# The last product of each layer in quarters (token half by column half), with gates and late attention blocks moved into existing memory

## The chip, the cores and the metric

One core of a Trainium2 chip runs the whole program. The metric is the time of one execution on the device in microseconds; lower is better. TensorE appears as PE (its weight loads as PEld), VectorE as DVE, ScalarE as ACT, GpSimd as POOL, and SyncE, which issues every DMA here, as SP.

## The reference

Two layers, each with a 1024 x 1024 residual stream (1024 tokens, width 1024), and a final RMSNorm. Cut to what matters:

```python
def hybrid_layer(x, c_act, norm_g, w_ada, b_ada, w_in, w_out, pos):
    shift, scale, gate = jnp.split(c_act @ w_ada + b_ada, 3, axis=-1)
    h = rms_norm(x, norm_g) * (1.0 + scale[:, None, :]) + shift[:, None, :]
    rq, rk, rv, rg, sq, sk, sv, sg = jnp.split(h @ w_in, split_at, axis=-1)   # 8 x 512 columns
    y_ret = retention(rotary(rq), rotary(rk), rv)           # 4 heads x 128
    y_ret = merge_heads(y_ret) * jax.nn.silu(rg)
    y_sb = stick_breaking(sq, sk, sv)                       # 8 heads x 64, strictly causal
    y_sb = merge_heads(y_sb) * jax.nn.silu(sg)
    y = jnp.concatenate([y_ret, y_sb], axis=-1) @ w_out
    return x + gate[:, None, :] * y
```

The stick-breaking attention multiplies, for a query t and a key s, sigmoid(q.k) by the product of (1 - sigmoid(q.k)) over the keys between s and t: a running product over keys, from the query backwards.

## The kernel before

**Arithmetic.** Every large product is done in three float16 passes, high x high, high x low and low x high (`three`, L605), each 128 x 128 by 512 columns. A tile of output takes 8 pieces of depth (k) times three passes, 24 matmuls. Activations live as `hh` and `hl` (high and low), weights as tiles `w` of 8 per group.

**Layer.** `layers` (L1124) goes through four head pairs: `stick_project` gives queries, keys, values and gates of two stick-breaking heads, `retention_project` one retention head in 8 token blocks with its chunk recurrences. Then `out_project` (L1002) multiplies the concatenated `y` with W_out: first the left 512 columns (hf = 0) for the token tiles t = 0 to 7, then the right 512 (hf = 1) for t = 0 to 7. `residual` (L1037) scales by the gate row, adds to the residual x on DVE and stores to DRAM; `finish` (L1108) normalises a complete row, and `h_chunk` turns four token tiles into `hh` and `hl` of the next layer. The matmuls of tile t need `("yr", l, k, t)` for k below 4, and for k from 4 on `("ys", l, k - 4, t // 4)`: the attention output of head pair k - 4 for that half of the tokens. `ys` of the second half exists only when query blocks 4 to 7 of that pair are through.

**Attention.** `attend` (L732) takes the eight blocks b of 128 queries of one head pair. For a block, PE forms the scores `z`, ACT the two sigmoids `beta` and `keep`, DVE runs for either head j a scan over the keys (`keep`), a product (`beta`) and, after ACT has copied the high part, a subtraction for the low part (`head_block`, L779); SP then issues transposing DMAs of `keep` into `ta`. `weigh` (L822) multiplies `ta` with the values into `av`, two blocks at a time (0 and 1, 2 and 3, 4 and 5, 6 and 7), and the half's result times its gate `sg` becomes `y`. A block with b of 4 or more needs four of the six `f4` buffers (`room4`), so blocks 4 to 7 follow each other closely in the same buffers.

**Order.** There is no fixed schedule: the generators above run in a planner (`Flow`) which keeps a priced clock per engine and always advances the stream of the lowest rank (DRAIN first, MAIN last) that can go on. What it emits is the static order of each engine's instructions; on the chip an engine takes them in that order and waits on semaphores. `Room` objects count buffers: `roomw` weight tiles (13), `roomst` staging tiles of loaded weights (3), `roomfl` value buffers (2), `rooms` the gates `sgs` (2). A weight tile is loaded into staging, split into high and low by ACT and DVE, and given back when the group's last tile has read it. A line L83 in the profile is the recorder through which all instructions pass, so tiles and shapes tell them apart.

## Time and profile before

| | |
|---|---|
| median of 3 runs | 1134.33 us (1131.88 to 1135.35) |
| the profiled execution's own time | 1132.87 us |
| its span, first to last instruction | 1131.0 us |
| PE busy | 1040.9 us, 92% of the span |
| DVE busy | 891.7 us, 79% |
| ACT busy | 553.1 us, 49% |
| POOL busy | 261.8 us, 23% |
| mean granted clock of TensorE | 0.983 of full |

The profiled execution lies 1.46 us below the median, and 1.87 us of it lie outside the span. Full granted clock is 2.4 GHz, 0.50 is 1.2 GHz. Layer 0's last product begins at 483.9 us of the span, layer 1's at 1011.1; the latter ends the program.

### The profile page before, as it was taken

What the parts mean: (1) busy time and instruction counts of PE and PEld (TensorE: products, weight loads), DVE (VectorE), ACT (ScalarE), POOL (GpSimd) and SP (SyncE); (2) the same over time, 40 slices, a digit from 0 to 9 for tenths busy, and PEclk for the clock granted to TensorE, in tenths of its full rate; (3) what the DMA queues carried; (4) which work ended last, traced back from release to release, by engine and by line L of the source; (5) the groups of instructions that cost most, each with busy time, mean ns of one, the idle gap of its engine ahead of it and who ended that gap; (6) DMA issues with size and microseconds to landing.
All of it is one profiled execution on the core that took longest, in us unless ns stands there. A gap on an engine that the chain in (4) does not pass through costs nothing. (4 is left out here: it accounts for less than half of the span.)

```text
span 1131.0 us, 18382 instructions
## 1 busy us (share of the span) xinstructions
PE 1040.9 (92%) x6321; PEld 506.3 (45%) x6321; DVE 891.7 (79%) x1689; ACT 553.1 (49%) x1271; POOL 261.8 (23%) x567
## 2 busy tenths in 40 slices
PE   1799989999999999996999999999999999999597
PEld 0444444454444444543455444444444544444343
DVE  6888888899898878975457689988978987887344
ACT  5755554545454646451254555555545464454012
POOL 5731430142014301420010034014302420230002
PEclk9899999999999999998999999999999999999799
DMA  9727675776774756374651566674556365467354
GB/s 279 234 65 154 140 152 132 183 143 157 162 171 89 145 90 140 61 185 114 207 153 57 128 146 137 149 150 82 134 107 124 72 143 109 97 143 168 81 186 162
DMA packets 339164, 156.44 MB, mean 138 GB/s; under 512 B 227904, under 2 KB 315008, under 8 KB 339072
## 3 DMA queue, kind: packets, MB, share of 16 engines
q1 hardware_dynamic: 339072, 155.29, 58.4%
q8 instruction: 49, 0.80, 0.3%
q14 instruction: 43, 0.35, 0.1%
HBM read 90.22 MB, written 10.49 MB: 89 GB/s over the span
## 5 line engine op out<-in xcount | busy, mean ns | idle before, releaser
L83 PE MATMUL acc<-hh,w 128*128 128x512 f16 x1024 | 324.2, 382 | 4.4 <-DVE w L83 3.2
L83 PE MATMUL acc<-w,hh 128*128 128x512 f16 x1024 | 305.0, 379 | 0.0
L83 PEld LDWEIGHTS <-w 128*128 128x128 f16 x1536 | 145.9, 99 | 183.8 <-issue 19.6
L83 POOL TENSOR_TENSOR t<-t,t 128x128 f32<-128x128 f32 (+1 forms) x192 | 137.3, 729 | 264.2 <-DVE t L83 205.3
L83 PE MATMUL acc<-hl,w 128*128 128x512 f16 x512 | 195.8, 382 | 0.9 <-POOL hl L83 0.9
L83 PE MATMUL acc<-w,hl 128*128 128x512 f16 x512 | 194.0, 379 | 0.0
L83 PE MATMUL acc<-w,y 128*128 128x512 f16 (+1 forms) x792 | 170.2, 373 | 3.3 <-ACT y L83 2.9
L83 PEld LDWEIGHTS <-hh 128*128 128x128 f16 x1024 | 92.6, 98 | 99.4 <-issue 11.4
L83 DVE SCALAR_TENSOR_TENSOR w<-wst,w 128x512 f16<-128x512 f32 x160 | 113.0, 722 | 28.2 <-ACT w L83 27.8
L83 DVE TENSOR_TENSOR_SCAN keep<-keep,own 128x640 f32<-128x640 f32 (+3 forms) x64 | 122.8, 1923 | 11.1 <-ACT keep L83 11.0
L83 ACT ACTIVATE w<-wst 128x512 f16<-128x512 f32 x160 | 97.7, 627 | 65.5 <-DMA wst<-in_w_in_dram 32.6
L83 PEld LDWEIGHTS <-y 128*128 128x128 f16 x792 | 76.2, 98 | 90.3 <-ACT y L83 3.4
L83 ACT CAST t<-t 128x128 f16<-128x128 f32 (+1 forms) x128 | 43.9, 352 | 108.3 <-POOL t L83 60.3
L83 ACT CAST keep<-beta 128x640 f16<-128x640 f32 (+3 forms) x64 | 56.3, 883 | 65.3 <-DVE beta L83 64.9
L83 PE MATMUL av<-ta,vt 128*64 128x256 f16 (+1 forms) x960 | 61.5, 280 | 26.8 <-DMA ta<-keep 26.7
L83 ACT ACTIVATE keep<-z 128x512 f32<-128x512 f32 (+3 forms) x128 | 67.8, 529 | 24.1 <-PE z L83 20.5
L83 PEld LDWEIGHTS <-hl 128*128 128x128 f16 x512 | 50.1, 98 | 60.4
L83 DVE TENSOR_TENSOR keep<-beta,keep 128x640 f16<-128x640 f32 (+3 forms) x64 | 67.0, 1051 | 4.5 <-ACT keep L83 4.0
L83 PEld LDWEIGHTS <-vt 128*64 128x64 f16 x960 | 50.6, 117 | 41.6 <-issue 21.9
L83 ACT ACTIVATE beta<-z 128x512 f32<-128x512 f32 (+4 forms) x128 | 68.5, 535 | 0.0
L83 DVE SCALAR_TENSOR_TENSOR beta<-beta,keep 128x639 f32<-128x639 f32 (+3 forms) x64 | 67.2, 1056 | 0.2
L83 POOL MEMSET both<- 128x1 f32 x64 | 5.3, 97 | 253.9 <-DMA ta<-keep 93.0
(104 smaller groups left out, 1308.7 us busy)
## 6 DMA issues: line engine op xcount, KB each, us to landing
wst<-in_w_in_dram SPq DMA_DIRECT2D x128, 256.0 KB, 3.3
wst<-in_w_ada_dram SPq DMA_DIRECT2D x64, 256.0 KB, 3.1
wst<-in_w_out_dram SPq DMA_DIRECT2D x32, 256.0 KB, 3.4
xt<-x SPq DMA_DIRECT2D x24, 256.0 KB, 4.0
xt<-in_x_dram SPq DMA_DIRECT2D x8, 512.0 KB, 5.8
ada<-in_w_ada_dram SPq DMA_DIRECT2D x8, 512.0 KB, 7.2
ada<-in_w_ada_dram SPq DMA_DIRECT2D x4, 1024.0 KB, 9.2
turn<-in_rot_dram SPq DMA_DIRECT2D x64, 64.0 KB, 2.4
```

The source lines that it names most:

```text
L83: real(*args, **kw)
```

## The change

The last product goes in quarters: tiles 0 to 3 left columns, 0 to 3 right, 4 to 7 left, 4 to 7 right. Both column halves of W_out are resident for it: 16 weight tiles in place of 13, and 4 staging tiles in place of 3. The memory comes from three places. The gates `sg` lie in the part of `y` that their own head pair writes later, so the two `sgs` buffers and their `rooms` count are gone. The value buffer `fl` is single. And query blocks 5 and 6 of the last head pair (p = 3) keep their `beta` and `keep` in a tile `home` that takes the memory of `hh` (block 5) or `hl` (block 6), from the moment that all projections of the layer have been issued (`("through", l)`); the next layer's `h_chunk` waits for their transposes. A complete row of tiles 0 to 3 is no longer in SBUF when its second column half is done: `residual` stores both halves, and `again_whole` loads the row again and finishes it, once the last attention block has taken its buffers (`("taken", l, 3)`). The modulation of the layer (`adapt`: gate row, and in layer 0 the next layer's shift and scale) starts at a new rank SPARE, between ATTEND and MAIN, and is lifted to ADAPT after the second head pair's `stick_project`. The number and shapes of matmuls do not change; the planner's order does, over most of the program.

```diff
     def part(self, a):
         name = a.tensor.name
-        return (name, a.offset) if name in self.big else name
+        return (name, a.offset // self.grain.get(name, 1)) if name in self.big else name
...
+    def lift(self, gen, rank):
+
+        for s in self.streams:
+            if s[2] is gen:
+                s[0] = rank
...
-DRAIN, NORM, FEED, ADAPT, ATTEND, MAIN = range(6)
+DRAIN, NORM, FEED, ADAPT, ATTEND, SPARE, MAIN = range(7)
...
-    N4, NW, NA = 6, 13, 2
-    room4, roomq, roomv, rooms = Room(N4), Room(2), Room(2), Room(2)
+    N4, NW, NA = 6, 16, 2
+    room4, roomq, roomv = Room(N4), Room(2), Room(2)
     roomr, roomw, rooma = Room(3), Room(NW), Room(1)
-    roomfl, roomg, roomy = Room(2), Room(5), Room(2)
-    roomat, roomst, roomt, roomrot = Room(NA), Room(3), Room(4), Room(2)
+    roomfl, roomg, roomy = Room(1), Room(5), Room(2)
+    roomat, roomst, roomt, roomrot = Room(NA), Room(4), Room(4), Room(2)
...
-                st = f2("wst", "wst", 3)
+                st = f2("wst", "wst", 4)
...
-            fl = wk.tile([P, 2, CH], F16, tag="fl", bufs=2, name="fl")
+            fl = wk.tile([P, 2, CH], F16, tag="fl", bufs=1, name="fl")
...
-            sg = wk.tile([P, CH], F32, tag="sgs", bufs=2, name="sg")
+
+            sg = y_of(l)[:, 4 + p, 4 * ch:4 * ch + 4].rearrange("p t a q -> p (t a q)").bitcast(F32)
...
                 acc = yield from project(3, ch, ch == 1)
-                yield (), rooms.has()
-                rooms.n -= 1
                 drain(3, ch, acc)
...
-            yield need, room4.has(2 if b < 4 else 4)
-            room4.n -= 2 if b < 4 else 4
-            flow.spawn(ATTEND, head_pair(l, p, b, at))
+            home = None
+            if p == 3 and b in (5, 6):
+
+                yield [*need, ("through", l)]
+                home = apart(big.tile([P, 4, 1024], F32, tag=("hh", "hl")[b - 5], name="home"))
+                flow.grain[home.tensor.name] = 1024
+            else:
+                yield need, room4.has(2 if b < 4 else 4)
+                room4.n -= 2 if b < 4 else 4
+            flow.spawn(ATTEND, head_pair(l, p, b, at, home))
             if b == 0:
                 flow.spawn(ATTEND, weigh(l, p, at))
+        flow.mark(("taken", l, p))
...
+        elif home is not None:
+            betas, keeps = [home[:, j] for j in range(2)], [home[:, 2 + j] for j in range(2)]
...
-    def out_project(l, hf, xres, xnew, fg):
+    def out_project(l, xres, xnew):
...
+        if last:
+            flow.spawn(NORM, final_row(), [("taken", l, 3)], room4.has())
+        for t0, hf in ((0, 0), (0, 1), (4, 0), (4, 1)):
+            g = ("O", l, hf)
+            fs = slice(hf * 512, (hf + 1) * 512)
+            yield [("w", g, 0)]
+            w = W[g]
+            for t in range(t0, t0 + 4):
+                whole = hf and t0
+                if whole:
+                    xt = yield from whole_tile(l, t)
+                    sp.dma_start(out=xt[:, 0:512], in_=xnew[t][:, 0:512])
+                    sp.dma_start(out=xt[:, 512:], in_=xres[t][:, fs])
+                    xs = xt[:, 512:]
                 else:
...
+                    xs = f2("xh")
+                    sp.dma_start(out=xs, in_=xres[t][:, fs])
...
+                flow.spawn(DRAIN, residual(l, hf, t, acc, xs, xt if whole else None, xnew), [acc, xs])
...
+    def whole_tile(l, t):
+        last = l == DEPTH - 1
+        if t < 6 or last:
+            yield [("taken", l, 3), *(["final"] if last else [])], room4.has()
+            room4.n -= 1
+            return f4("xt")
...
-        yield [xs], None, None, LOADED if hf == 0 else 0
-        if hf == 0 or l + 1 < DEPTH:
+        yield [xs], None, None, LATER if xt is None else 0
+        if xt is None or l + 1 < DEPTH:
             sp.dma_start(out=xnew[t][:, fs], in_=xs)
...
+        elif hf:
+            flow.spawn(NORM, again_whole(l, t, xnew), [("x", l, t, i) for i in range(2)])
+
+    def again_whole(l, t, xnew):
+        xt = yield from whole_tile(l, t)
+        sp.dma_start(out=xt, in_=xnew[t])
+        yield [xt]
+        yield from finish(l, t, xt)
...
-                    flow.spawn(NORM, h_chunk(l + 1, t // 4, [xns[t - 3 + j] for j in range(4)], i, n))
+                    flow.spawn(NORM, h_chunk(l + 1, t // 4, [xns[t - 3 + j] for j in range(4)], i, n),
+                               [("at", l, 3, b, j) for b in (5, 6) for j in range(2)])
...
                 if i == 0:
-                    flow.spawn(ADAPT, adapt(l))
+                    rest = adapt(l)
+                    flow.spawn(SPARE, rest)
+                if i == 1:
+                    flow.lift(rest, ADAPT)
                 yield from retention_project(l, i)
...
+            flow.mark(("through", l))
             xnew = (x1, x2)[l]
-            for hf in range(2):
-                yield from out_project(l, hf, xres, xnew, fg)
+            yield from out_project(l, xres, xnew)
```

**PE, last product of layer 1, at the end of token tile 3.** `acc` is a tile's accumulator, `w_11261` and `w_11916` are the first and the last left-column weight tile before, `w_11255` the last left-column tile and `w_11866` the first right-column tile in the changed kernel. Before:

```order
L83 MATMUL acc_12257<-w_11916,y_7315 128x512
L83 LDWEIGHTS y_7315
L83 MATMUL acc_12290<-w_11261,y_7315 128x512
L83 LDWEIGHTS y_7315
L83 MATMUL acc_12290<-w_11261,y_7315 128x512
```

Changed:

```order
L83 MATMUL acc_12231<-w_11255,y_7018 128x512
L83 LDWEIGHTS y_7018
L83 MATMUL acc_12267<-w_11866,y_7018 128x512
L83 LDWEIGHTS y_7018
L83 MATMUL acc_12267<-w_11866,y_7018 128x512
```

The accumulator that follows tile 3 is tile 4, left, before, and tile 0, right, in the changed kernel. The 21 matmuls of tile 4, left, that need no second-half attention still stand directly ahead of the last weighted sum (`av` from blocks 6 and 7) in both kernels; in the changed one four right-column tiles (96 matmuls) stand ahead of them.

**DVE, layer 0, the end of the attention of the last head pair.** `keep_6071`/`keep_6072` before and `keep_6038`/`keep_6039` in the changed kernel belong to query block 7, heads 0 and 1; `home_5834` is block 6; the `up` and `xh` pair is the residual of the `acc` that it names. Before:

```order
L83 SCALAR_TENSOR_TENSOR up_6141<-acc_6047,gate_948 128x512
L83 TENSOR_TENSOR xh_6045<-xh_6045,up_6141 128x512
L83 SCALAR_TENSOR_TENSOR keep_6071<-keep_6071,own_76 128x1024
L83 SCALAR_TENSOR_TENSOR beta_6069<-beta_6069,keep_6071 128x1023
L83 SCALAR_TENSOR_TENSOR up_6178<-acc_6137,gate_948 128x512
L83 TENSOR_TENSOR xh_6135<-xh_6135,up_6178 128x512
L83 TENSOR_TENSOR keep_6071<-beta_6069,keep_6071 128x8x128
L83 SCALAR_TENSOR_TENSOR keep_6072<-keep_6072,own_76 128x1024
L83 SCALAR_TENSOR_TENSOR beta_6070<-beta_6070,keep_6072 128x1023
L83 TENSOR_TENSOR keep_6072<-beta_6070,keep_6072 128x8x128
```

Changed:

```order
L83 SCALAR_TENSOR_TENSOR keep_6038<-keep_6038,own_76 128x1024
L83 SCALAR_TENSOR_TENSOR up_6240<-acc_6159,gate_961 128x512
L83 TENSOR_TENSOR xh_6157<-xh_6157,up_6240 128x512
L83 SCALAR_TENSOR_TENSOR beta_6036<-beta_6036,keep_6038 128x1023
L83 SCALAR_TENSOR_TENSOR keep_6039<-keep_6039,own_76 128x1024
L83 SCALAR_TENSOR_TENSOR up_6278<-acc_6236,gate_961 128x512
L83 TENSOR_TENSOR xh_6234<-xh_6234,up_6278 128x512
L83 SCALAR_TENSOR_TENSOR beta_6037<-beta_6037,keep_6039 128x1023
L83 TENSOR_TENSOR keep_6038<-beta_6036,keep_6038 128x8x128
L83 TENSOR_TENSOR keep_6039<-beta_6037,keep_6039 128x8x128
L83 SCALAR_TENSOR_TENSOR up_6323<-acc_6274,gate_961 128x512
L83 TENSOR_TENSOR xh_6272<-xh_6272,up_6323 128x512
```

Block 7's passes are in both; in the changed kernel the residuals between them are those of right-column tiles (`acc_6159`, `acc_6236` and `acc_6274` are tiles 1, 2 and 3), and block 6's last pass stands directly ahead. Counting back to the last retention block's first pass, the changed kernel has all passes of blocks 4, 5, 6 and 7 in this stretch, before only part of 6 and all of 7; the other passes of 4 to 6 stood earlier.

**SP, layer 0, the last transposes.** `ta` is filled from `keep` for the last weighted sum; `x1` is the DRAM copy of the residual. Before:

```order
L83 DMA x1_83<-xh_6135 128x512
L83 DMA_TRANSPOSE ta_5996<-keep_6071 128x8x128 x2
L83 DMA_TRANSPOSE ta_6144<-keep_6072 128x8x128 x2
L83 DMA xh_6265<-in_x_dram 128x512
L83 DMA x1_83<-xh_6172 128x512
```

Changed:

```order
L83 DMA x1_83<-xh_6157 128x512
L83 DMA xh_6272<-in_x_dram 128x512
L83 DMA xt_6291<-x1_83 128x1024
L83 DMA x1_83<-xh_6234 128x512
L83 DMA_TRANSPOSE ta_6214<-keep_6038 128x8x128 x2
L83 DMA xh_6317<-in_x_dram 128x512
L83 DMA xt_6338<-x1_83 128x1024
L83 DMA x1_83<-xh_6272 128x512
L83 DMA_TRANSPOSE ta_6249<-keep_6039 128x8x128 x2
```

Before, the four transposes of block 7 stand together. In the changed kernel head 1's two stand behind a store of `xh_6272` (tile 3, right) and behind two reloads of whole rows of `x1` (`xt_6291`, `xt_6338`).

## Rows read from the trace of the kernel before

**Rows 1.** Busy time by engine in two stretches (granted clock, DMA share, GB/s last)

```profile
75.00:500.00 425.00, 408.99 (x2582) 196.06 (x2581) 370.08 (x724) 222.86 (x539) 101.84 (x224) 1.00 0.63 137
575.00:1030.00 455.00, 448.67 (x2808) 217.16 (x2807) 379.47 (x737) 242.36 (x572) 101.24 (x231) 1.00 0.56 122
```

**Rows 2.** Timeline of PE in layer 0's last product: start, length, matmuls [idle before]

```profile
483.77 0.33 PE L83 MATMUL psc<-vd,t 128*128 128x128 f16 x3
...
520.14 0.42 PE L83 MATMUL av<-ta,vt 128*64 128x256 f16 x1 [2.63 <-DMA ta<-keep]
525.98 0.37 PE L83 MATMUL av<-ta,vt 128*64 128x256 f16 x2 [5.42 <-DMA ta<-keep]
527.20 3.92 PE L83 MATMUL av<-ta,vt 128*64 128x128 f16 x45 [0.85 <-DMA ta<-keep]
532.56 27.66 PE L83 MATMUL acc<-w,y 128*128 128x512 f16 x126 [1.44 <-ACT y L83]
```

**Rows 3.** Timeline of PE in layer 1's last product, same columns

```profile
1011.09 0.81 PE L83 MATMUL acc<-w,y 128*128 128x512 f16 x3
...
1022.40 2.35 PE L83 MATMUL av<-ta,vt 128*64 128x256 f16 x36
...
1025.67 13.76 PE L83 MATMUL acc<-w,y 128*128 128x512 f16 x63
1039.36 0.82 PE L83 MATMUL z<-k,q 64*128 64x512 f16 x6
...
1054.28 0.37 PE L83 MATMUL av<-ta,vt 128*64 128x256 f16 x1 [10.54 <-DMA ta<-keep]
1057.10 0.42 PE L83 MATMUL av<-ta,vt 128*64 128x256 f16 x2 [2.44 <-DMA ta<-keep]
1058.30 4.59 PE L83 MATMUL av<-ta,vt 128*64 128x128 f16 x45 [0.79 <-DMA ta<-keep]
1064.33 16.01 PE L83 MATMUL acc<-w,y 128*128 128x512 f16 x72 [1.43 <-ACT y L83]
```

**Rows 4.** Busy time by engine in two stretches of 12.5 us, columns as Rows 1

```profile
520.00:532.50 12.50, 4.71 (x48) 3.90 (x48) 2.23 (x3) 1.66 (x2) 0.00 (x0) 0.60 0.36 76
1050.00:1062.50 12.50, 4.99 (x46) 4.38 (x47) 2.14 (x2) 0.86 (x1) 0.00 (x0) 0.50 0.50 105
```

**Rows 5.** Timeline of DVE, layer 0: last retention block's first pass, last attention pass

```profile
489.03 0.75 DVE L83 TENSOR_TENSOR t<-acc,turn 128x256 f32<-128x256 f32 x2
...
521.48 1.23 DVE L83 TENSOR_TENSOR keep<-beta,keep 128x1024 f16<-128x1024 f32 x1 [1.17 <-ACT keep L83]
```

**Rows 6.** Timeline of DVE, layer 1: the same two places

```profile
1012.10 0.76 DVE L83 TENSOR_TENSOR t<-acc,turn 128x256 f32<-128x256 f32 x2 [0.20 <-DVE yt L83]
...
1049.78 2.36 DVE L83 TENSOR_TENSOR keep<-beta,keep 128x1024 f16<-128x1024 f32 x2
```

**Rows 7.** DVE instructions by shape: total busy, mean ns | idle before

```profile
L83 DVE SCALAR_TENSOR_TENSOR w<-wst,w 128x512 f16<-128x512 f32 x160 | 113.0, 722 | 28.2 <-ACT w L83 27.8
...
L83 DVE TENSOR_TENSOR_SCAN keep<-keep,own 128x1024 f32<-128x1024 f32 x16 | 36.4, 2283 | 9.3 <-ACT keep L83 9.3
...
L83 DVE TENSOR_TENSOR_SCAN keep<-keep,own 128x640 f32<-128x640 f32 x16 | 25.2, 1572 | 1.0 <-ACT keep L83 1.0
...
L83 DVE SCALAR_TENSOR_TENSOR up<-acc,gate 128x512 f32<-128x512 f32 x31 | 21.3, 688 | 37.4 <-PE acc L83 37.3
...
L83 DVE SCALAR_TENSOR_TENSOR beta<-beta,keep 128x1023 f32<-128x1023 f32 x16 | 19.3, 1216 | 0.1
L83 DVE TENSOR_TENSOR keep<-beta,keep 128x1024 f16<-128x1024 f32 x16 | 19.3, 1215 | 1.5 <-ACT keep L83 1.3
...
L83 DVE SCALAR_TENSOR_TENSOR beta<-beta,keep 128x639 f32<-128x639 f32 x16 | 13.6, 854 | 0.0
```

**Rows 8.** DMA issues: count, KB each, median us from issue to landing

```profile
x<-xh SPq DMA_DIRECT2D x16, 256.0 KB, 2.2
...
vt<-fl SPq DMA_TRANSPOSE x16, 2.7
```

More of the change, by code (lines that the diff above doesn't have):

```diff
@@ L110, in __init__ @@
         self.big = set()
+        self.grain = {}
         self.bank = {}
@@ L727, in stick_project @@
                 acc = yield from project(3, ch, ch == 1)
-                yield (), rooms.has()
-                rooms.n -= 1
                 drain(3, ch, acc)
@@ L774, in head_pair, with head_block @@
                 if s0 + w == n:
-                    flow.spawn(ATTEND, head_block(l, p, b, j, at, betas[j], keeps[j]))
+                    flow.spawn(ATTEND, head_block(l, p, b, j, at, betas[j], keeps[j], home))
         if b == NT - 1:
             roomq.n += 1
-    def head_block(l, p, b, j, at, beta, keep):
+    def head_block(l, p, b, j, at, beta, keep, home):
         n = (b + 1) * P
@@ L795, in head_block @@
         if b >= 4:
-            room4.n += 1
+            room4.n += home is None
         if b + j:
@@ L999, in retain @@
             roomy.n += 1
-    def out_project(l, hf, xres, xnew, fg):
+    def out_project(l, xres, xnew):
         y = y_of(l)
         last = l == DEPTH - 1
-        g = ("O", l, hf)
-        fs = slice(hf * 512, (hf + 1) * 512)
-        yield [("w", g, 0)]
-        w = W[g]
-        for t in range(NT):
-            if hf:
-                if t < 6 or last:
-                    yield (), room4.has()
-                    room4.n -= 1
-                    xt = f4("xt")
-                else:
-                    yield (), roomq.has(0.5)
-                    roomq.n -= 0.5
-                    xt = wk.tile([P, D], F32, tag="qk", bufs=4, name="xt")
-                sp.dma_start(out=xt[:, 0:512], in_=xnew[t][:, 0:512])
-                sp.dma_start(out=xt[:, 512:], in_=xres[t][:, fs])
-                xs = xt[:, 512:]
-            else:
-                yield (), roomt.has()
-                roomt.n -= 1
-                xs = f2("xh")
-                sp.dma_start(out=xs, in_=xres[t][:, fs])
-            if last and hf and t == NT - 1:
-                yield from final_tile(g, xt, fg)
-                continue
-            acc = bank("acc", "pj", 2)
-            yield from three(acc, lambda k: y[:, k, t, 0], lambda k: y[:, k, t, 1],
-                             lambda k: w[k][:, 0], lambda k: w[k][:, 1],
-                             lambda k: [("w", g, k), ("gate", l),
-                                        ("yr", l, k, t) if k < 4 else ("ys", l, k - 4, t // 4)], t == NT - 1)
-            flow.spawn(DRAIN, residual(l, hf, t, acc, xs, xt if hf else None, xnew, fg), [acc, xs])
@@ L1037, in residual @@
-    def residual(l, hf, t, acc, xs, xt, xnew, fg):
+        if last:
[12 more added lines that the diff above has]
+                    xs = xt[:, 512:]
+                else:
+                    yield (), roomt.has()
+                    roomt.n -= 1
+                    xs = f2("xh")
+                    sp.dma_start(out=xs, in_=xres[t][:, fs])
+                if last and whole and t == NT - 1:
+                    yield from final_tile(g, xt)
+                    continue
+                acc = bank("acc", "pj", 2)
+                yield from three(acc, lambda k: y[:, k, t, 0], lambda k: y[:, k, t, 1],
+                                 lambda k: w[k][:, 0], lambda k: w[k][:, 1],
+                                 lambda k: [("w", g, k), ("gate", l),
+                                            ("yr", l, k, t) if k < 4 else ("ys", l, k - 4, t // 4)], t == NT - 1)
+                flow.spawn(DRAIN, residual(l, hf, t, acc, xs, xt if whole else None, xnew), [acc, xs])
@@ new lines, in trunk, with final_row @@
+    final = []
+    def final_row():
+        room4.n -= 1
+        final.append(f4("fg"))
+        sp.dma_start(out=final[0], in_=final_g.rearrange("(o d) -> o d", o=1).broadcast_to([P, D]))
+        flow.mark("final")
+        yield ()
+    def whole_tile(l, t):
+        last = l == DEPTH - 1
+        if t < 6 or last:
+            yield [("taken", l, 3), *(["final"] if last else [])], room4.has()
+            room4.n -= 1
+            return f4("xt")
+        yield (), roomq.has(0.5)
+        roomq.n -= 0.5
+        return wk.tile([P, D], F32, tag="qk", bufs=4, name="xt")
@@ L1038, in residual @@
+    def residual(l, hf, t, acc, xs, xt, xnew):
         fs = slice(hf * 512, (hf + 1) * 512)
@@ L1043, in residual, with final_tile @@
         dve.tensor_add(xs, xs, up)
-        yield [xs], None, None, LOADED if hf == 0 else 0
-        if hf == 0 or l + 1 < DEPTH:
+        yield [xs], None, None, LATER if xt is None else 0
+        if xt is None or l + 1 < DEPTH:
             sp.dma_start(out=xnew[t][:, fs], in_=xs)
-        if not hf:
+            flow.mark(("x", l, t, hf))
+        if xt is None:
             roomt.n += 1
-        if hf:
-            flow.spawn(NORM, finish(l, t, xt, fg), [xt])
-    def final_tile(g, xt, fg):
-        l, y, w = DEPTH - 1, y_of(DEPTH - 1), W[g]
+        if xt is not None:
+            flow.spawn(NORM, finish(l, t, xt), [xt])
+        elif hf:
[5 more added lines that the diff above has]
+        yield from finish(l, t, xt)
+    def final_tile(g, xt):
+        l, y, w, fg = DEPTH - 1, y_of(DEPTH - 1), W[g], final[0]
         t = NT - 1
@@ L1131, in layers @@
                 if i == 0:
-                    flow.spawn(ADAPT, adapt(l))
+                    rest = adapt(l)
+                    flow.spawn(SPARE, rest)
+                if i == 1:
+                    flow.lift(rest, ADAPT)
                 yield from retention_project(l, i)
-            fg = None
-            if last:
-                yield (), room4.has()
-                room4.n -= 1
-                fg = f4("fg")
-                sp.dma_start(out=fg, in_=final_g.rearrange("(o d) -> o d", o=1).broadcast_to([P, D]))
+            flow.mark(("through", l))
             xnew = (x1, x2)[l]
-            for hf in range(2):
-                yield from out_project(l, hf, xres, xnew, fg)
+            yield from out_project(l, xres, xnew)
             xres = xnew
```

14 lines of the change are left out of this document (6 added, 8 removed).

## The prediction

> **What bounds the kernel now.** I read the stages first: in the two long stretches PE is busy 409.0 of 425 us and 448.7 of 455, DVE 370 and 379 [rows 1]. PE sets the time there, with 16.0 and 6.3 us of small waits; DVE has little room in layer 0 (87%). Then I read PE's timeline where a layer ends, because a change of the last product acts there. The reader should see one pattern twice. PE issues the first four tiles and 21 matmuls of tile 4, then stands until the transposes of the last attention blocks have landed (`av <- DMA ta`), does the weighted sum, stands once more for `y`, and goes on. In layer 0 the four waits are 2.63, 5.42, 0.85 and 1.44, together 10.3 us [rows 2]; in layer 1 they are 10.54, 2.44, 0.79 and 1.43, together 15.2 us [rows 3]. Third, the clock: the granted share is 0.60 and 0.50 in the 12.5 us around these waits, and PE's 4.71 and 4.99 us of work there ran mostly at half rate [rows 4]; half of it, 2.4 and 2.5 us, is lost too. So a layer's end costs 12.7 and 17.7 us. Who ends the waits is DVE's attention passes: the last one ends at 522.7 in layer 0 [rows 5] and at 1052.1 in layer 1 [rows 6], and the bulk of the weighted sum begins 4.5 and 6.2 us later [rows 2, 3], which is the transposes' issue and landing.
>
> **The change: the cover.** No matmul is added or removed. Four right-column tiles, 96 matmuls, come ahead of the wait. One costs 13.76 / 63 = 0.218 us [rows 3], so 21.0 us of work stand where PE idled 8.9 and 13.8. If the data came when it comes now, both waits would be gone. It does not come then: blocks 5 and 6 may only start when all projections have been issued, so DVE has more left when the last product begins. Both sides must be added up, from the end of the last retention accumulator (call it zero) to the last weighted sum, by the order of the changed kernel.
>
> *PE, layer 0:* 213 product matmuls 46.5; 24 full score matmuls at 0.82 for six and 18 shorter ones, at most 5.7 in all; 60 of weighted sums at 2.35 / 36, 3.9; 27 retention matmuls at 0.33 for three, 3.0 [rows 2, 3]: 59. I checked the prices on the kernel before: the same sum gives 32.5 for its stretch, and from 483.8 to the first wait at 517.5 went 33.7, a factor of 1.04 that holds small waits; the shorter scores are priced high. So PE arrives at about 60. *Layer 1:* 213 again, fewer weighted sums (36) and scores: 57.0; there the check gives 33.2 for the 32.7 that passed up to the first wait at 1043.7, so 56.
>
> *DVE, layer 0:* a block's three passes for one head cost 2.28 + 1.22 + 1.22 = 4.71 at 1024 keys and 1.57 + 0.85 + 0.85 = 3.3 at 640 [rows 7], in a straight line 3.8 and 4.2 between. Blocks 4 to 7, two heads: 32.0. Seven residuals of two passes at 0.69: 9.6. Seven weight splits at 0.72: 5.1. One `y`: 1.4. Eighteen small retention passes at about 0.33: 5.9. Sum 54.0. The check: passes of before priced so give 33.0 and 33.7 went by [rows 5], so 55.1. DVE began 5.3 us after zero there (489.0 against 483.8) [rows 2, 5]. *Layer 1:* block 4 is already through at zero; blocks 5 to 7 25.4, residuals 9.6, eight splits 5.8, 24 small passes 7.9: 48.8, and DVE began only 1.0 late there [rows 3, 6].
>
> **What is left of the waits.** Layer 1: data at 1.0 + 48.8 + 4.5 to 6.2 = 54 to 56, PE at 56. The wait goes; I leave 1 us, and the 1.4 us for `y`, which nothing new covers. No half rate. 17.7 - 2.4 = **15.3 gained**. Bounds: if DVE starts as late as in layer 0, 2.5 to 4.2 us of waiting return and the clock's 2.5 with it, so 9.6; at best only `y` stays, 16.3.
>
> Layer 0: data at 5.3 + 55.1 + 4.5 to 6.2, and 1.4 more, because head 1's transposes stand on SP behind the store of tile 3's right residual, which DVE makes after the last attention pass: 66 to 68 against PE's 60. With DVE starting 1 us late, as in layer 1, it is 62 to 64. I take a wait of 6, nearer to layer 0's own row; the `y` wait of 1.4 stays (eight transposes of the next layer's input may fill half of it); of the clock I take 1.5 of 2.4, as the wait is shorter. 12.7 - 8.9 = **3.8 gained**; bounds 0.9 (a wait of 8, the whole clock term) and 11.3 (no wait). Late next is what DVE had to put off, and there is nothing behind it on PE that could run: tile 4 onward needs that half of `y`.
>
> The clock term against the skill: the row shows 0.60 over a stretch whose idle came in pieces of 2.63, 5.42 and 0.85 us [rows 4, 2]. The Trainium skill (TensorE: Matmul & The Clock Gate, part 1, What's actually happening) says that half rate is the default, that activity alone lifts it, and that idling brings it back. By that rule layer 0's remaining wait would bring back all 2.4, and the whole would come out at 1116, not 1115.
>
> **The other edits.** The 16th weight tile and fourth staging tile: the right-column tiles are all split after 18 us of DVE's passes in layer 0, 24 us after zero, and PE wants the first after some 30, so they cost nothing; if that cover failed, each late tile would cost its split, 0.7 us. The next layer's first weights can be loaded only from tile 7, left, on, 96 matmuls (21 us) before they are wanted; their splits take 8 x 0.72 = 5.8 us of DVE in that time, hidden by DVE's room there. The reloads of rows 0 to 3 and the norms after them lie beside the 42 us of tiles 4 to 7. The moved modulation and the freed gates change the order in the long stretches; no row prices that. All 16.0 and 6.3 us of waits there could shrink, and DVE's postponed passes could add as much; from row to row I see no sign, so 0, and 6 us either way.
>
> **Sum.** 15.3 + 3.8 = 19.1 off the profiled execution's 1132.87 gives 1113.8; the median is 1.46 higher: **1115 us**.
>
> **Rivals.** *Both waits go* (chance 0.20): DVE starts layer 0's stretch early, since it has had less to do before it. Speaks for it: the passes of blocks 4 to 6 have left the busy stretch. Against: DVE's own 54 us. Gain 11.3 + 16.3: 1107.
>
> *DVE holds both ends* (0.20): layer 0 keeps its cost, layer 1 gains only 9.6: 1125. For it: DVE at 87% in layer 0 [rows 1], and passes that wait for ACT. Against: layer 1's start 1.0 late.
>
> *SP holds the transposes* (0.07). Two reloads of rows just stored stand ahead of head 1's transposes in layer 0, two more in layer 1. A store lands after 2.2 us [rows 8]; if SP stands for that before each reload, and DVE does not take longer anyway, 4.4 us are added: 1119. Against: DVE has five passes, 7.3 us, between the first such store's data and the transposes' data, and 5.0 at the second. The Trainium skill (DMA: Bandwidth & Descriptors, Two DMAs through the same engine are not ordered) asks for just this wait on the issuing engine.
>
> *Slower* (0.08): the single value buffer. A buffer is bound for the landing of 2.7 us [rows 8] and for whatever SP stands at ahead of it; the next values come three products later, 3 x 24 x 0.218 = 15.7 us. Only if SP keeps a transpose past about 18 us is the accumulator held and PE stopped; to end 0.3% slower all 16 transposes would have to cost 22.5 / 16 = 1.4 us each. Nothing in the trace points there, but the order of the whole middle is new.
>
> **Chances and range.** The forecast has 0.45. What a measurement can tell from no change is 0.3%, 3.4 us, here 1131 to 1138. The forecast, both-go and SP cases lie clear of it, the DVE case mostly: faster 0.87, the same 0.05, slower 0.08. The forecast with 6 us either way is 1109 to 1121; for eight in ten it must take in both-go with some of the long stretches' waits and the DVE case with a loss there: 1103 to 1130.
>
> **What would show it.** Right: in layer 1 the wait for `ta` ahead of the last weighted sum falls from 13.8 to a few us and the granted clock stays at 1.00 around it; in layer 0 one wait of some 6 us stays there, its last pass on DVE ending some 60 us after the last retention accumulator; 96 more matmuls stand ahead of both. Waits in the long stretches stay near 16 and 6. Wrong: the wait in layer 1 stays above 5 us, the next layer's first product waits for `w`, PE waits for the accumulators that values hold, or the long stretches move by more than 6 us.

## The result, and the profile after

The changed kernel takes 1107.9 us, median of three runs (1104.1, 1107.4, 1108.4; a fourth execution, of 2169.8, took about twice as long and is left out, as is one of 2023.6 in e7 below), against 1134.5: a ratio of 0.976, 95% interval 0.973 to 0.979. The forecast was 1115, range 1103 to 1130. The profiled executions differ by more: 1104.09 against 1132.87, which is 28.8 us where the sum had 19.1.

The two long stretches after, in the columns of [rows 1]:

```profile
75.00:500.00 425.00, 420.35 (x2623) 201.28 (x2621) 375.71 (x738) 229.22 (x555) 98.47 (x226) 0.99 0.63 142
575.00:1030.00 455.00, 447.49 (x2785) 214.34 (x2783) 373.49 (x725) 237.23 (x566) 96.85 (x228) 1.00 0.55 121
```

Layer 0's stretch holds 4.7 us without TensorE's work, not 16.0; in both kernels the stretch is the same 425 us. Layer 1's holds 7.5, before 6.3. The ends of the layers, PE's timeline after (start, length, matmuls, idle before), first layer 0, to be read beside [rows 2]:

```profile
469.41 0.33 PE L83 MATMUL psc<-vd,t 128*128 128x128 f16 x3
...
508.74 17.66 PE L83 MATMUL acc<-w,y 128*128 128x512 f16 x81
526.32 0.30 PE L83 MATMUL av<-ta,vt 128*64 128x256 f16 x1
530.95 0.42 PE L83 MATMUL av<-ta,vt 128*64 128x256 f16 x2 [4.33 <-DMA ta<-keep]
531.85 4.74 PE L83 MATMUL av<-ta,vt 128*64 128x128 f16 x45 [0.48 <-DMA ta<-keep]
536.52 1.21 PE L83 MATMUL pht<-ident,xt 128*128 128x128 f32 x8
538.03 0.60 PE L83 MATMUL acc<-w,y 128*128 128x512 f16 x2 [0.29 <-ACT y L83]
538.81 0.39 PE L83 MATMUL acc<-w,y 128*128 128x512 f16 x1 [0.17 <-DVE y L83]
```

then layer 1, beside [rows 3]:

```profile
1030.64 18.95 PE L83 MATMUL acc<-w,y 128*128 128x512 f16 x87
1049.52 0.30 PE L83 MATMUL av<-ta,vt 128*64 128x256 f16 x1
1050.49 0.30 PE L83 MATMUL av<-ta,vt 128*64 128x256 f16 x2 [0.67 <-DMA ta<-keep]
1051.44 2.51 PE L83 MATMUL av<-ta,vt 128*64 128x128 f16 x45 [0.66 <-DMA ta<-keep]
1056.65 3.71 PE L83 MATMUL acc<-w,y 128*128 128x512 f16 x15 [2.69 <-ACT y L83]
```

The new cover is seen in the x81 and x87, the last pieces of products ahead of the last weighted sum (tile 4's 21 left-column products are among them). Layer 1's waits for `ta` are 0.67 and 0.66 where they were 10.54, 2.44 and 0.79; the wait for `y` grew from 1.43 to 2.69. Layer 0 keeps a wait of 4.33 and one of 0.48, and the 45 matmuls behind it take 4.74 us, in layer 1 2.51. The clock in the stretches around (third number from the end; [rows 4] before):

```profile
525.00:537.50 12.50, 7.69 (x63) 5.92 (x61) 0.85 (x2) 5.88 (x8) 1.67 (x5) 0.73 0.63 167
1050.00:1062.50 12.50, 8.54 (x73) 4.86 (x74) 6.22 (x7) 2.82 (x6) 2.22 (x6) 1.00 0.93 309
```

0.73 and 1.00, before 0.60 and 0.50. Last, what stood ahead of that wait of 4.33: DVE's last attention pass of layer 0 ([rows 5] before), and SyncE's queue at that place:

```profile
470.62 0.75 DVE L83 TENSOR_TENSOR t<-acc,turn 128x256 f32<-128x256 f32 x2
...
519.81 2.49 DVE L83 TENSOR_TENSOR keep<-beta,keep 128x1024 f16<-128x1024 f32 x2
```

```profile
521.06 2.61 SPq L83 DMA_TRANSPOSE ta<-keep  x2
523.72 0.58 SPq L83 DMA_DIRECT2D xh<-in_x_dram  x1
524.41 0.38 SPq L83 DMA_DIRECT2D xt<-x  x1
524.83 0.43 SPq L83 DMA_DIRECT2D x<-xh  x1
525.36 4.43 SPq L83 DMA_TRANSPOSE ta<-keep  x2
```

Head 1's data was there at 522.30 and head 0's transposes had left the queue at 523.67, but head 1's were issued at 525.36, behind a load, a reload and a store.

For the comparison of all kernels I divided each profiled span where its own last products begin, and took the stage's length less PE's busy time in it. That is PE's idle time, in us, of one profiled execution each; that of e2 lies 4.3 us above its median ("end" runs from the last product's start: to 575 us in layer 0, to the span's end in layer 1; "`ta`" sums PE's waits for the transposes in the whole span). Each version's label is explained below. Where a run speaks of the idle time before 325 us, it is counted from 75 us; it was 10.6 before and is 3.1 in the changed kernel.

| kernel | median | 75 us to last product, layer 0 | end, layer 0 | 575 us to last product, layer 1 | end, layer 1 | `ta` | clock |
|---|---|---|---|---|---|---|---|
| before | 1134.5 | 13.8 | 12.7 | 6.3 | 23.9 | 26.8 | 0.983 |
| changed | 1107.9 | 4.0 | 6.0 | 5.8 | 14.1 | 6.2 | 0.988 |
| e1 modulation early | 1103.8 | 5.6 | 5.1 | 4.0 | 15.4 | 3.8 | 0.988 |
| e2 blocks not postponed | 1128.4 | 5.7 | 17.6 | 9.6 | 18.2 | 9.1 | 0.979 |
| e3 three staging tiles | 1094.8 | 2.5 | 3.8 | 4.8 | 14.9 | 5.3 | 0.997 |
| e4 order by halves | 1128.0 | 6.9 | 18.4 | 3.8 | 25.4 | 30.8 | 0.978 |
| e5 before, 16 weight tiles | 1142.7 | 15.0 | 16.6 | 6.9 | 27.5 | 46.4 | 0.973 |
| e6 before, gates in outputs | 1131.0 | 8.4 | 20.0 | 4.5 | 24.5 | 29.6 | 0.983 |
| e7 before, both | 1131.6 | 4.1 | 22.9 | 1.9 | 35.0 | 46.3 | 0.980 |
| e8 e1 and e3 together | 1100.1 | 4.2 | 6.4 | 1.3 | 18.5 | 6.2 | 0.988 |
| e9 last transposes first | 1106.0 | 5.1 | 4.6 | 7.5 | 14.2 | 2.4 | 0.987 |
| e10 two value buffers | 1109.9 | 4.9 | 5.9 | 6.7 | 14.7 | 5.1 | 0.984 |
| e11 e3 and e9 together | 1084.5 | 3.2 | 2.9 | 2.6 | 11.7 | 0.6 | 0.995 |
| e12 order disturbed | 1119.8 | 5.6 | 14.5 | 6.8 | 15.5 | 3.1 | 0.981 |

From before to the changed kernel, idle time fell by 9.8 us in layer 0's long stretch, which the forecast had taken as nothing, by 6.7 and 9.8 at the ends and by 0.5 between.

### The profile page after: what moved, and what is told of

Its sections match the earlier page's. It is cut to its first block, busy times and chain, and to the rows that moved or that the text cites. A ratio compares the mean times of both kernels' runs of the same rounds, so it can differ in the third digit from the quotient of the medians.

```text
span 1102.3 us, 18360 instructions
## 1 busy us (share of the span) xinstructions
PE 1037.9 (94%) x6321; PEld 505.8 (46%) x6321; DVE 891.9 (81%) x1689; ACT 553.0 (50%) x1271; POOL 253.5 (23%) x567
## 5 line engine op out<-in xcount | busy, mean ns | idle before, releaser
L83 POOL TENSOR_TENSOR t<-t,t 128x128 f32<-128x128 f32 (+1 forms) x192 | 129.0, 687 | 231.4 <-DVE t L83 182.6
L83 DVE SCALAR_TENSOR_TENSOR w<-wst,w 128x512 f16<-128x512 f32 x160 | 113.9, 733 | 15.3 <-ACT w L83 14.8
L83 DVE TENSOR_TENSOR_SCAN keep<-keep,own 128x640 f32<-128x640 f32 (+3 forms) x56 | 106.7, 1909 | 11.0 <-ACT keep L83 11.0
L83 ACT ACTIVATE w<-wst 128x512 f16<-128x512 f32 x160 | 96.4, 629 | 26.3 <-DMA wst<-in_w_in_dram 18.5
L83 DVE TENSOR_TENSOR t<-acc,turn 128x256 f32<-128x256 f32 x128 | 48.0, 416 | 27.4 <-ACT vd L83 26.6
L83 ACT ACTIVATE keep<-z 128x512 f32<-128x512 f32 (+3 forms) x112 | 59.3, 530 | 20.7 <-PE z L83 20.3
L83 PE MATMUL z<-k,q 64*128 64x512 f16 (+3 forms) x576 | 65.0, 326 | 1.7 <-ACT home L83 1.1
L83 ACT CAST keep<-beta 128x640 f16<-128x640 f32 (+3 forms) x56 | 49.4, 884 | 34.2 <-DVE beta L83 34.0
L83 DVE TENSOR_TENSOR keep<-beta,keep 128x640 f16<-128x640 f32 (+3 forms) x56 | 58.1, 1040 | 6.3 <-ACT keep L83 6.3
L83 PE MATMUL av<-ta,vt 128*64 128x256 f16 (+1 forms) x960 | 57.1, 270 | 6.2 <-DMA ta<-keep 6.1
L83 ACT ACTIVATE beta<-z 128x512 f32<-128x512 f32 (+4 forms) x112 | 59.9, 535 | 0.0
```

Of the source, the lines that this page charges most:

```text
L83: real(*args, **kw)
```

## The experiments

The question was where the 9.8 us came from, and which part earns the ends. The first four undo one part of the change each.

**e1: the modulation at its old rank**

```diff
-                    rest = adapt(l)
-                    flow.spawn(SPARE, rest)
-                if i == 1:
-                    flow.lift(rest, ADAPT)
+                    flow.spawn(ADAPT, adapt(l))
```

> The changed kernel with the modulation spawned at its old rank at once, the rest kept. The surplus of the gain lies in layer 0's long stretch: TensorE's gaps between 75 us and the start of layer 0's last product fell from 13.8 to 4.0 us, and 7.4 of these 9.8 us fell before 325 us, ahead of the postponed blocks. Theory M (the moved modulation frees VectorE there): the gaps before 325 us come back from 3.2 to about 10 us, time about 1115 us. Theory S (the fourth staging tile): gaps before 325 us stay at 3 to 4 us, time 1108 us within 2. Theory H (the postponed blocks): the same as S here.

Measured: 1103.8 us, ratio 0.974 (0.971 to 0.976), 4 us faster than the changed kernel; idle before 325 us 4.4. Theory M falls: the moved modulation earned nothing that comes back when it is undone.

**e2: blocks 5 and 6 in the ring again**

```diff
-            if p == 3 and b in (5, 6):
+            if False:
```

> The changed kernel with blocks 5 and 6 of the last head pair in the ring of six tiles as before, not behind the last projection; the rest kept. Theory M or S: the gaps up to 325 us stay at 3 us; only the stretch from 325 us to the last product gives back up to the 2.4 us by which it fell (0.8 now, 3.2 before), and the ends lose the cover of these blocks, some 3 us of VectorE's passes a layer: about 1112 us. Theory H: the 9.0 us of VectorE's work that no longer stand ahead of the last product make the surplus: the gaps from 75 us to the last product come back to about 13 us, and the time is about 1118 us.

Measured: 1128.4 us, 0.995 (0.993 to 0.996). Neither number was right. The stretch up to the last product keeps 5.7 us of idle time, so theory H falls for that stretch; but the end of layer 0 loses far more than the 3 us of passes that were expected there. PE's timeline of this version:

```profile
538.05 0.47 PE L83 MATMUL pht<-ident,xt 128*128 128x128 f32 x1 [5.98 <-ACT xt L83]
539.10 0.48 PE L83 MATMUL pht<-ident,xt 128*128 128x128 f32 x1 [0.57 <-ACT xt L83]
544.55 1.33 PE L83 MATMUL pht<-ident,xt 128*128 128x128 f32 x5 [4.97 <-ACT xt L83]
545.80 4.91 PE L83 MATMUL av<-ta,vt 128*64 128x256 f16 x48
```

The transposes of the next layer's input (`pht`) are written ahead of the last weighted sum, and PE stands 5.98, 0.57 and 4.97 us for rows that have to be reloaded and scaled; the weighted sum itself then runs without a wait. The run e12 shows below that this place in the order can come about without any change of parts, so these 11.5 us can't be put down to the blocks.

**e3: three staging tiles**

```diff
-    roomat, roomst, roomt, roomrot = Room(NA), Room(4), Room(4), Room(2)
+    roomat, roomst, roomt, roomrot = Room(NA), Room(3), Room(4), Room(2)
...
-                st = f2("wst", "wst", 4)
+                st = f2("wst", "wst", 3)
```

> The changed kernel with three staging tiles instead of four, the rest kept. Theory S: ScalarE's waits on staged weights come back (18.5 to about 32 us), the waits of a projection's products on a split weight come back by 2.1 us and gaps before 325 us to about 8 us: time about 1114 us. Theories M and H: gaps before 325 us stay below 5 us, time 1108 to 1110 us.

Measured: 1094.8 us, 0.965 (0.963 to 0.967), idle before 325 us 1.9. Theory S falls; with less staging it was faster. Of the 11.0 us between the two spans, 8.9 are PE's busy time (1037.9 against 1029.1, the sums over the stages), that is, the clock: 0.997 against 0.988.

**e4: the last product by halves again**

```diff
-        for t0, hf in ((0, 0), (0, 1), (4, 0), (4, 1)):
+        for t0, hf in ((0, 0), (4, 0), (0, 1), (4, 1)):
-                whole = hf and t0
+                whole = hf
```

> The changed kernel with its last product by feature halves again (all eight tokens' left half, then all eight right halves); weights resident, gates in the outputs' memory and postponed blocks kept. If the order by quarters makes the gain at the ends: layer 1's end gets back most of its 11 us (waits and the clock's loss, 15.2 + 2.5 before, about 4 + 0.7 now), layer 0's end some 6 us, and the time is about 1124 us; the long stretches stay as they are. Rival: the postponed blocks and the resident weights alone cover the passes of the end, and the time stays under 1112 us.

Measured: 1128.0 us, 0.994 (0.992 to 0.996). Layer 0's end on PE:

```profile
519.10 0.42 PE L83 MATMUL av<-ta,vt 128*64 128x256 f16 x1 [10.09 <-DMA ta<-keep]
522.66 0.42 PE L83 MATMUL av<-ta,vt 128*64 128x256 f16 x2 [3.14 <-DMA ta<-keep]
523.91 4.75 PE L83 MATMUL av<-ta,vt 128*64 128x128 f16 x45 [0.83 <-DMA ta<-keep]
```

The waits for `ta` are back, longer than before (10.09 + 3.14 + 0.83; layer 1's are 9.84, 3.16 and 0.89), since the postponed blocks come late and nothing stands ahead of their sum. The rival falls: without the quarters the other parts leave these waits uncovered. Layer 0's end holds 12.4 us more idle time than in the changed kernel, twice the 6 that were expected. The table bears out layer 1's part: its end holds 11.7 to 18.5 us in all nine versions with the quarters, and 23.9 to 35.0 in the five without.

All four kept the long stretch of layer 0 below 7 us. So the next three put what they share into the kernel before.

**e5: the kernel before with sixteen weight tiles**

```diff
-    N4, NW, NA = 6, 13, 2
+    N4, NW, NA = 6, 16, 2
...
-    roomfl, roomg, roomy = Room(2), Room(5), Room(2)
+    roomfl, roomg, roomy = Room(1), Room(5), Room(2)
...
-            fl = wk.tile([P, 2, CH], F16, tag="fl", bufs=2, name="fl")
+            fl = wk.tile([P, 2, CH], F16, tag="fl", bufs=1, name="fl")
```

> The kernel before with sixteen weight tiles (and one buffer of value tiles, which makes their room), nothing else. Four variants of the changed kernel kept the gaps of 75 to 325 us at 1.9 to 5.4 us (10.6 before) without the postponed blocks, the moved modulation, the fourth staging tile or the quarter order, so what they share must do it: the sixteen weight tiles, or the gates in the outputs' memory. Theory W (the weight tiles): the three waits of a projection's products on a split weight (2.1 us) go, and the gaps of 75 to 325 us fall to 3 to 6 us; the ends stay; time about 1127 us. Theory G (the gates): the gaps stay at 9 to 11 us, time 1132 to 1137 us.

Measured: 1142.7 us, 1.007 (1.005 to 1.009). The waits on split weights went, but the long stretch holds 12.2 us of waits for `ta` (3.5 before). Sixteen tiles with a single value buffer don't make the fall; sixteen tiles with two value buffers, as e7 has them, were not run by themselves.

**e6: the kernel before with the gates in the outputs' memory**

```diff
-            sg = wk.tile([P, CH], F32, tag="sgs", bufs=2, name="sg")
+            sg = y_of(l)[:, 4 + p, 4 * ch:4 * ch + 4].rearrange("p t a q -> p (t a q)").bitcast(F32)
...
-                    yield (), rooms.has()
-                    rooms.n -= 1
...
```

> The kernel before with the gates kept in the outputs' memory and the two gate buffers with their waits gone, nothing else. Theory G: a projection's last column no longer stands until the pair before has been weighed, products are there to put into waits, and the gaps of 75 to 325 us fall from 10.6 to 3 to 6 us: about 1127 us. Theory W: the gaps stay at 9 to 11 us and the time at 1132 to 1137 us. If neither does it alone, both stay there and the next run alone falls.

Measured: 1131.0 us, 0.996 (0.995 to 0.998); idle before 325 us 7.6, between the two theories, and 8.4 up to the last product (13.8 before). Waits on split weights are still there, 2.8 us.

**e7: both** (with the value buffers at two, as before)

> The kernel before with both: gates in the outputs' memory and sixteen weight tiles; last product by halves, blocks and modulation as before. By W and G alike the gaps of 75 us to the last product fall from 13.8 to about 5 us, and the time is about 1126 us, with the two ends as before (gaps 12.7 and 23.9 us to the span's end). Rival: the fall of the gaps comes from another order of the program that each of these edits happens to bring; then the gaps stand anywhere between 4 and 14 us and follow neither edit.

Measured: 1131.6 us, 0.996 (0.995 to 0.998). The long stretch now holds 4.1 us of idle time, and the last products begin 18.1 and 13.2 us earlier than before (465.86 against 483.94, 997.84 against 1011.09). The time hardly moves, because the attention blocks follow only in part: the bulk of the last weighted sum begins at 520.94 and 1056.56, 6.3 and 1.7 us earlier than in [rows 2, 3]. The longest waits of the two ends on PE:

```profile
516.79 0.42 PE L83 MATMUL av<-ta,vt 128*64 128x256 f16 x1 [15.66 <-DMA ta<-keep]
...
1052.49 0.37 PE L83 MATMUL av<-ta,vt 128*64 128x256 f16 x1 [18.82 <-DMA ta<-keep]
```

15.66 and 18.82 us, where the kernel before waits 5.42 and 10.54 [rows 2, 3]. The eleven versions that have both parts hold 2.5 to 6.9 us in layer 0's long stretch, in ten different orders, the three without both 8.4 to 15.0, so chance alone is an unlikely rival for this stretch. With the quarters added (the changed kernel against e4), the waits at the ends go and the earlier start becomes time.

**e8: e1 and e3 together**

> The changed kernel with three staging tiles and the modulation at its old rank, the two undone parts that came out no slower (1094.8 and 1103.8 us against 1107.9). If each is a gain of its own, about 1091 us. If the 13 us of the three tiles are the clock alone (8.9 of them are TensorE's busy time, with a granted clock of 0.997 against 0.988, and only 2.1 us are gaps), the order of this version may lose them again: between 1092 and 1106 us, with a clock between 0.985 and 0.998.

Measured: 1100.1 us, 0.969 (0.967 to 0.971), clock 0.988: slower than e3 alone, inside the 1092 to 1106 of the second case. The two don't add.

**e9: the last block's transposes ahead in SyncE's queue**

```diff
-            yield [keep, *order]
+            yield [keep, *order], None, None, -8000 if p == 3 and b == NT - 1 else 0
```

> The changed kernel with one number added in the order: the transposes of a layer's very last attention block are put out ahead of what is queued beside them, so that in layer 0 head 1's stand right behind head 0's on SyncE, not behind a load of x, a reload and a store. Their data was there at 522.3 us, head 0's left the queue at 523.7, and head 1's were issued at 525.4. Theory Q (the queue holds what is left of layer 0's wait): the wait of 4.3 us falls by 1.6 to about 2.7; if that keeps the clock up, the 45 matmuls behind it take 2.5 instead of 4.7 us too: 1104 to 1106 us against 1107.9. Theory D (VectorE and the landing hold it): the wait stays above 3.8 us and the time within 1 us.

Measured: 1106.0 us, 0.975 (0.973 to 0.978). PE at layer 0's end, and the transposes on SyncE:

```profile
528.80 0.30 PE L83 MATMUL av<-ta,vt 128*64 128x256 f16 x1
529.71 0.27 PE L83 MATMUL av<-ta,vt 128*64 128x256 f16 x2 [0.61 <-DMA ta<-keep]
530.99 2.51 PE L83 MATMUL av<-ta,vt 128*64 128x128 f16 x45 [1.02 <-DMA ta<-keep]
535.80 4.53 PE L83 MATMUL acc<-w,y 128*128 128x512 f16 x12 [2.29 <-ACT y L83]
```

```profile
523.54 5.43 SPq L83 DMA_TRANSPOSE ta<-keep  x4
```

Theory Q holds at its place: all four transposes go out in one piece, the wait of 4.33 us is 0.61, the next 1.02, and the 45 matmuls run at full rate, 2.51 us. Little else moved: only 50 of PE's 6321 matmuls stand in another place than in the changed kernel, and DVE's last attention pass ends 52.4 us after the last product's start in the changed kernel, 52.3 here. But of the 5.4 us so won, 2.0 go at once to the wait for `y` (2.29, before 0.29). The eight transposes of the next input that filled 1.2 of it are no longer there, and `y` itself comes some 0.9 us later after the sum. About 1.9 more go to the clock, which falls behind this wait: the 12 products take 4.53 us, which at 0.218 are 2.6, and the granted clock of the stretch is 0.66.

```profile
535.00:540.00 5.00, 4.20 (x12) 1.43 (x13) 2.08 (x3) 3.04 (x6) 0.88 (x3) 0.66 0.61 204
```

By PE's 3200th matmul, 102.7 us after the last product's start (105.2 in the changed kernel), 2.4 us of the gain are left, all small pieces taken together. The runs of the changed kernel lie up to 4.3 us apart, so the whole time can't show them.

**e10: two value buffers, nothing else**

> The changed kernel with two buffers of value tiles as before; every engine's order stays the same, row for row. The rival that priced a slower outcome: the single buffer holds accumulators and stops TensorE. If it does at all, this version is faster by what it waits for them; the page of the changed kernel shows no such wait, so I expect 1107.9 within 2 us. This run also shows what two kernels of the same order differ by.

Measured: 1109.9 us, 0.977 (0.975 to 0.980). The order is the same row for row, and PE's wait of 4.33 is 4.32 here. The slower rival falls: a single buffer costs nothing that can be seen. The 2 us are what two kernels of one order differ by; layer 1's wait for `y` is 4.28 us here, where the changed kernel has 2.69.

**e11: e3 and e9 together**

> The fastest version so far (three staging tiles, 1094.8 us) with the last transposes ahead as in the run of their own. Its waits in layer 0's end are 0.3 and 0.7 us already, so theory Q gives it nothing there; layer 1's order moves with it. Within 3 us of 1094.8 if the order of layer 1 is no matter; above 1098 us if that version's place was owed to its particular order.

Measured: 1084.5 us, 0.957 (0.954 to 0.959): the fastest of all, 10 us below e3, which neither side expected. The weighted sums of its two ends, on PE:

```profile
519.20 0.35 PE L83 MATMUL av<-ta,vt 128*64 128x256 f16 x3
520.10 2.51 PE L83 MATMUL av<-ta,vt 128*64 128x128 f16 x45 [0.56 <-DMA ta<-keep]
...
1033.01 2.65 PE L83 MATMUL av<-ta,vt 128*64 128x256 f16 x48
```

In layer 1 the sum of 48 matmuls runs without any wait. In e3 it stood there for 3.29 and 0.56 us, and the 45 matmuls took 3.90:

```profile
1039.43 0.30 PE L83 MATMUL av<-ta,vt 128*64 128x256 f16 x2 [3.29 <-DMA ta<-keep]
1040.28 3.90 PE L83 MATMUL av<-ta,vt 128*64 128x128 f16 x45 [0.56 <-DMA ta<-keep]
```

That is some 5 us at this place. But of the 8.5 us between the two spans 4.1 were there when layer 1's last product began (975.91 against 980.04), and layer 0's waits for these transposes can't have held them: they were 0.95 us in e3 and are 0.56 here. From layer 0's end on the order differs in 1510 of PE's matmuls, and the run doesn't separate that from the queue.

**e12: the order disturbed, the parts kept**

```diff
-LOADED = 400
+LOADED = 450
```

> A control for the order itself: the changed kernel with a constant of the planner, the time it allows behind a load, at 450 ns instead of 400. Nothing is added, removed or resized; the written order changes in most of its rows, as it did with three staging tiles (1094.8) and with the modulation at its old rank (1103.8). If those differences are what the parts are worth, this stays at 1108 within 3 us. If they are the order's chance, it lands anywhere between 1095 and 1115 us, with the clock and small waits making the difference.

Measured: 1119.8 us, 0.987 (0.984 to 0.990): 12 us slower than the changed kernel with the same parts, and outside the 1095 to 1115 that the order's chance was given. 2614 of PE's 6321 matmuls stand in another place. PE at layer 0's end:

```profile
527.45 0.33 PE L83 MATMUL pht<-ident,xt 128*128 128x128 f32 x1 [0.73 <-ACT xt L83]
531.84 0.48 PE L83 MATMUL pht<-ident,xt 128*128 128x128 f32 x1 [4.07 <-ACT xt L83]
536.73 1.33 PE L83 MATMUL pht<-ident,xt 128*128 128x128 f32 x5 [4.41 <-ACT xt L83]
537.99 3.49 PE L83 MATMUL av<-ta,vt 128*64 128x256 f16 x48
```

As in e2, transposes of the next input stand ahead of the weighted sum, and PE waits 0.73, 4.07 and 4.41 us for reloaded rows. This one place in the written order holds 9.2 us. All parts are those of the changed kernel, so it is the order that put it there; but the rows that PE waits for are the reloads of complete rows, which the change brought in and the prediction priced at nothing.

## Why the prediction was right, point by point

The measured 1107.9 lies inside the stated range, but below the forecast's own band of 1109 to 1121: the range reached down to 1103 for another case. The mechanism at the ends held, and the long stretches brought what the forecast had at 0.

**The waits of layer 1.** Forecast: 1 us left of 13.8 and the whole `y` wait of 1.4, no half rate. Measured: 1.33 and 2.69, clock 1.00. From the last product's start at 992.97, PE took 56.9 us up to the first wait in the sum (forecast 56) and the data 57.5 (54 to 56). The waits fell by 11.2 (15.2 to 4.0) and the 45 matmuls by 2.1 (4.59 to 2.51): 13.3 against 15.3. e4 shows that the quarter order does it. The misses are the `y` wait, taken as unchanged (why it grew wasn't tried), and two new waits of 0.80 and 0.82 us in that end for the postponed blocks (`home`), which no term held; with them the end's idle time fell by 9.8, not 11.2.

**The waits of layer 0.** Forecast: 6 us left, then 1.4 and 1.5 of clock. Measured: 4.33 + 0.48, then 0.29 + 0.17. PE came at 526.6, 57.2 us after the last retention product at 469.41 (forecast 60), the data at 530.95, after 61.5 (forecast 66 to 68). DVE began 1.2 us after that point, not 5.3, which is the case of "62 to 64" that the prediction named and did not take. Its passes took 51.7 us, not 55.1, so the last one ended 52.9 us after zero where "some 60" was to be the sign. From its end to the data went 8.7 us, where 4.5 to 6.2 and 1.4 were counted. That the transposes stand behind others in SyncE's queue was counted with the 1.4; by e9 it was the larger part of the wait. So the rival "SP holds the transposes" named the right place and was no slower case. Its reason was another: SyncE did stand 1.7 us for a store's landing, but ahead of a reload at 518.60 and before DVE's data was there.

The clock term of layer 0 was wrong in sign: the 45 matmuls took 4.74 us, before 3.92. Its size was over-read too: against 2.51 at full rate they had lost 1.4 us before, where the prediction halves all 4.71 us of PE's work in a stretch of clock 0.60. The Trainium skill (TensorE: Matmul & The Clock Gate, part 1, What's actually happening) says that idling brings half rate back; the trace agrees, half rate after 4.33 us of idle time here, full rate after 0.61 and 1.02 in e9 and half rate after the 2.29 that followed. The prediction's sentence by that rule, that all of the clock's loss would come back, was nearer than its own term. In sum 10.3 - 5.3 - 0.8 = 4.2, against 3.8. That this agrees is luck: the waits fell by 5.1 where 2.9 were forecast, the clock lost 0.8 where it was to win 0.9, and the wait itself came out near 6 because errors cancelled: PE's arrival, DVE's start and DVE's passes were put 3 to 4 us too late or too long, and the way from DVE to the data 1 to 3 us too short.

**The term that was mis-sized.** The ends came to 13.3 + 4.2 = 17.5 against 19.1. The step that failed is "The moved modulation and the freed gates change the order in the long stretches; no row prices that [...] so 0, and 6 us either way", with the sentence ahead of it that the sixteenth weight tile and the fourth staging tile "cost nothing". The idle time up to the last product fell by 9.8 us in layer 0 and by 0.5 in layer 1; by the prediction's own rows 16.0 became 4.7, in layer 0, which is its sign of being wrong, "the long stretches move by more than 6 us". e1 rules out the modulation, e3 the staging, e2 and e4 the blocks and the quarters; e7 shows that freed gates and weight tiles together do it. Gates alone take 13.8 to 8.4 (e6), and the tiles with a single value buffer leave 15.0 (e5); that buffer made no such difference in the changed kernel (4.0 with one, 4.9 with two in e10). How they do it is argued only: with thirteen tiles products waited for split weights (2.1 us before, 2.8 in e6, none in e5 and e7), and with gate buffers a pair's last column is held until an earlier pair was weighed.

**The freed gates and tiles earn little without the quarters.** e7 gives 3 us and e4, with the postponed blocks added, 7. The cover of 21 us is what turns an earlier last product into time. The quarters without them were not run, since both column halves of W_out take the sixteen tiles. The prediction priced cover and stretches as separate terms; in e7 the earlier last products came with longer waits at the ends (57.9 us of idle time there, before 36.6), and the cover is worth 25 us of waits then (30.8 in e4, 6.2 with the quarters).

**The rivals.** "DVE holds both ends" falls with layer 1's 0.67. "Both waits go" (1107) has the right time for another reason: layer 0's wait stayed. The value buffer falls by e10.

**What stays open.** How much of 26.6 us is the parts and how much the order they happened to bring. The eight versions with all of gates, tiles, quarters and postponed blocks lie between 1084.5 and 1119.8, the six others, the kernel before among them, between 1128.0 and 1142.7. So the gain is real, but its size, from 15 to 50 us, is in good part the order's. The kernel before was not run in a disturbed order of its own. For the same reason the worth of the postponed blocks isn't settled: e2 is 20 us slower than the changed kernel, but 8.6 slower than e12, which has the same wait for `pht`.

## What to carry to other kernels

An engine's slack in one stage is not a gain until the stage behind it can take the work: look for what the last stage waits for before counting waits that vanish upstream, and make the cover first. Where a list scheduler writes the order, change a constant that stands for no part of the kernel and run that too; here it moved the time by 12 us, and smaller differences between the times of two versions say nothing of their parts. In the order, look first for an engine's queue on which something urgent stands behind something that can wait (a load, a store, the next layer's transposes).

## What the runs showed of the hardware that was not expected

Short waits can be followed by a loss of clock that is larger than the waits, and the same waits can leave the clock up. In the changed kernel PE waits 0.31 and 1.45 us in the middle of layer 0:

```profile
247.96 0.28 PE L83 MATMUL po<-vd,t 128*128 128x128 f16 x2 [0.31 <-ACT t L83]
249.70 0.23 PE L83 MATMUL po<-vd,t 128*128 128x128 f16 x1 [1.45 <-DVE t L83]
...
252.75 1.06 PE L83 MATMUL acc<-w,hh 128*128 128x512 f16 x2
```

Pairs of products take 1.06 us instead of 0.59 from then to 256.6 us; half of these 6.6 us, about 3.3, is lost beside 1.8 of waiting. The windows view of the stretch (granted clock third from the end):

```profile
245.00:250.00 5.00, 3.24 (x22) 1.60 (x21) 4.63 (x11) 1.82 (x8) 2.12 (x3) 1.00 0.12 26
250.00:255.00 5.00, 5.00 (x19) 2.79 (x18) 3.96 (x13) 1.73 (x4) 2.65 (x7) 0.50 0.66 148
```

In e4 PE waits 0.38 and 1.45 us at the same place, and the clock stays at 1.00:

```profile
250.00:255.00 5.00, 3.17 (x26) 2.00 (x24) 4.89 (x13) 1.04 (x4) 2.41 (x5) 1.00 0.23 52
255.00:260.00 5.00, 5.00 (x31) 2.18 (x30) 4.05 (x12) 2.62 (x7) 2.12 (x6) 1.00 0.84 205
```

So the length of such waits doesn't settle whether the clock falls; what does isn't shown by these runs. The waits at layer 0's end in e9, 0.61 and 1.02 us, left the clock up, and the next one, 2.29 us, was followed by half rate. And a pair of transposes of the same size held SyncE's queue for 2.61 us at 521.06 and for 4.43 at 525.36, behind three other DMAs; in e9 all four took 5.43.
